# Norms between two layers: column sums with Newton steps, or sums on all partitions with Ln and Exp

## The chip, the cores and the metric

The kernel runs on one core of a Trainium2 chip. The metric is the device time of one execution in microseconds (us); lower is better. Times of three runs are shown, and one further execution was taken with the hardware profiler, which gives the trace.

Engines are called by their names here and by short names in the rows: TensorE (PE for its matmuls, PEld for its weight loads), VectorE (DVE), ScalarE (ACT), GpSimd (POOL) and SyncE (SP), whose queue issues most transfers. L318 is line 318 of the kernel before.

## The reference

The model has two layers (L = 2) over 512 tokens with 1,024 features each. With the parts that matter here:

```python
for l in range(DEPTH):
    shift, scale, gate = jnp.split(c_act @ w_ada[l] + b_ada[l], 3, axis=-1)
    h = rms_norm(x, norm_g[l]) * (1.0 + scale) + shift
    z = h @ w_in[l]          # queries, keys, values, forget gates, latents, gates
    ...                      # forgetting attention on 8 heads, latent attention on 8 heads
    y = concatenate([y_fox, y_mla]) @ w_out[l]
    x = x + gate * y
return rms_norm(x, final_g)
```

`rms_norm` multiplies each token by 1/sqrt(mean of its 1,024 squares + 1e-6). So between the layers the kernel has to finish the new x of a token, sum its squares over all features, take the root, scale x, and only then can it begin with the second layer's products for that token. The same sum is needed once more at the very end, for the last norm.

## The kernel before

**Layout.** x is kept transposed: 8 tiles, each with 128 features on the partitions and 512 tokens along the columns. Everything is float32. A product is made of three reduced-precision ones (`mm3`, L238): high weight part by high input part (L239), high by low (L240), low by high (L241); which of the operands is the weight differs between the output projection and the v projection. Each weight tile is loaded raw by SyncE (L220), its high part is a cast on ScalarE (L124), its low part a subtraction on VectorE (L127). High and low parts live in rings of three buffers each, raw weights in a ring of two, so a cast waits until TensorE has let go of the tile three places earlier.

**Between the layers.** `project` (L947) runs the output projection. Its tiles n = 0 to 3 are done on all 512 tokens, tiles 4 to 7 first on the tokens of the first half (`HALF[0]`), then on those of the second half in the order 7, 6, 5, 4; tiles 5 and 4 are loaded and split a second time for that. `tile_n` (L953) loads the old x as residual (L956), does 24 products (8 k steps by 3), adds gate times y to the residual (L962, VectorE), stores the new x (L965), and squares it (L317, ScalarE) and adds the square into `acc` (L318, VectorE). `half_done` is called once for each half. In layer 0 it is `enter_second` (L1003), in layer 1 `finish` (L1031).

`enter_second` sums `acc` over the partitions with 128-column weight loads and a one-column moving operand (L1014), so the sums come out with tokens on partitions. `newton` (L346) takes the root in twelve small operations on VectorE, a copy (L352) widens the result, and `spread` (L356) brings it back along the columns with one product for each 128 tokens (L361). Then `h_chunk` (L380) makes the second layer's input for each of 8 feature tiles: L385 on VectorE, L388 (high part) on ScalarE, L389 (low part) on VectorE; in the text these are the chunk operations. For the second half the sums stand after one step of the second layer's v projection on the first half's tokens (`v_half`, L509; SUMS_AT = 1), and the spread after two more (SPREAD_AT = 2). A step of `v_half` takes a pair of weight tiles, two k values by two token blocks by three products, 12 in all.

`finish` does the same for the last norm in another way: a matrix of ones as the weights' partner, so that every partition gets each token's sum (L1034, and L1036 for the last tile's square, which is not added into `acc`), then Ln (L1038) and Exp (L1039) on ScalarE, then multiplies and output transfers.

**What sets the order.** Inside `mix` (attention and input projections) TensorE's order is written out by hand. Everywhere else, and on all other engines, a planner orders the instructions: it goes through a simulated time and takes, of those that are ready, the one that stands earliest in the program. `keep_in_program_order` puts an instruction behind the one that precedes it in the program on its engine; it does not hold later ones back. Each engine works its list strictly in order. ScalarE needs a table load when it goes to a function that its present table lacks: Ln and Exp have one together, Tanh and Exp another.

Of the kernel before, what the change touches and what calls it, by code (L numbers as in the profile page):

```python
# [13 lines left out]
AF = mybir.ActivationFunctionType  # L14
# [3 lines left out]
P = 128  # L18
D = 1024
# [3 lines left out]
L = 2  # L23
# [41 lines left out]
V_LO = ('pvpp','pppv',)  # L65
ROWS_U = {1: 2}
PRIO_W = 0
SUMS_AT, SPREAD_AT = 1, 2
PIN_ROWS = (0,2,3,)
PE_ENGINE = mybir.EngineType.PE  # L70
FIRST_W = 816
# [9 lines left out]
HALF = (slice(0, 256), slice(256, 512))  # L81
# [3 lines left out]
def trunk(ctx, tc, xT_in, pos, c_in, cols_in, w_first, w_proj, w_small, w_v, w_uq, w_ukv, w_out, ada_0, ada_r, out):  # L85
    nc = tc.nc
# [17 lines left out]
    def nm(s):  # L104
        uid[0] += 1
        return f"{s}_{uid[0]}"

    def scr(tag="scr", bufs=4, dt=F32, n=T):
        return wk.tile([P, n], dt, tag=tag, bufs=bufs, name=nm(tag))
# [4 lines left out]
    def bank(kind):  # L114
        pool = {"p": ps_p, "s": ps_s, "t": ps_t, "a": ps_a}[kind]
        return pool.tile([P, T], F32, tag=kind, name=nm("ps" + kind))
# [20 lines left out]
    ones = const.tile([P, P], F32, name="ones")  # L137
# [5 lines left out]
    for half in range(2):  # L143
        cs = slice(512 * half, 512 * half + 512)
# [4 lines left out]
    eps_c = const.tile([P, 1], F32, name="eps_c")  # L149
# [68 lines left out]
    def load_w(src, n=1024):  # L218
        raw = wp.tile([P, 1024], F32, tag="raw", bufs=R_BUFS, name=nm("raw"))
        nc.sync.dma_start(out=raw[:, :n], in_=src)  # L220
        return raw

    def split_w(src, n=1024, eng=None):
        return parts_w(load_w(src, n), n, eng)
# [3 lines left out]
    def parts_w(raw, n, eng=None):  # L228
        with prio(boost[0]):
            lo = wp.tile([P, 1024], F32R, tag="wl", bufs=W_BUFS, name=nm("wl"))  # L230
            hi = wp.tile([P, 1024], F32R, tag="wh", bufs=W_BUFS, name=nm("wh"))
            ins = hi_of(hi[:, :n], raw[:, :n])
            if hold[0] and "w" in PIN_S:
                behind(ins, hold[0], "after the forget gates")
            lo_of(lo[:, :n], raw[:, :n], hi[:, :n], eng)
        return hi, lo
# [89 lines left out]
    def newton_steps(sums, cs, width):  # L326

        n = (cs.stop - cs.start) // P
        q = wk.tile([P, 4, NT], F32, tag="nw", bufs=3, name=nm("nw"))
        m, a, y, t = (q[:, i, 0:n] for i in range(4))  # L330
        for i, src in enumerate(sums):
            c = n // len(sums)
            nc.vector.tensor_scalar(out=m[:, i * c:(i + 1) * c], in0=src, scalar1=1.0 / width, scalar2=EPS,
                                    op0=ALU.mult, op1=ALU.add)

        nc.vector.tensor_scalar(out=y.bitcast(I32), in0=m.bitcast(I32), scalar1=-0.5, scalar2=float(0x5F3759DF),
                                op0=ALU.mult, op1=ALU.add)
        nc.vector.tensor_scalar(out=a, in0=m, scalar1=-0.5, scalar2=None, op0=ALU.mult)
        for _ in range(3):
            yield  # L340
            nc.vector.tensor_mul(out=t, in0=y, in1=y)
            nc.vector.tensor_mul(out=t, in0=t, in1=a)
            nc.vector.scalar_tensor_tensor(out=y, in0=t, scalar=1.5, in1=y, op0=ALU.add, op1=ALU.mult)
        yield y

    def newton(sums, cs, width):  # L346
        *_, y = newton_steps(sums, cs, width)
        return y, widen(y, (cs.stop - cs.start) // P)
# [7 lines left out]
    def spread(rb, cs, here=False):  # L356

        ps = bank("t")
        for j in range((cs.stop - cs.start) // P):
            s = slice(cs.start + j * P, cs.start + (j + 1) * P)  # L360
            mm = nc.tensor.matmul(out=ps[:, s], lhsT=rb[:, j * P:(j + 1) * P], rhs=ident, start=True, stop=True)  # L361
            if here and j == 0:
                tc.keep_in_program_order(mm)
        return ps
# [3 lines left out]
    class Layer:  # L368
# [578 lines left out]
        def project(self, half_done):  # L947
            l = self.l
            self.x = [slot(self.s_x + n) for n in range(KC)]
            sq = Squares()  # L950
            res_in = xT_in if l == 0 else x_dram

            def tile_n(n, w, cs, kind):  # L953
                c = cs.stop - cs.start
                res = scr(tag="gate", bufs=3)
                nc.sync.dma_start(out=res[:, :c], in_=res_in[:, n, cs])  # L956
                if n in self.part:
                    ps, w = self.part[n]
                else:
                    ps = bank(kind)  # L960
                self.out_mms(ps[:, :c], w, cs, range(EARLY_K if n in self.part else 0, KC))
                nc.vector.scalar_tensor_tensor(out=self.x[n][:, cs], in0=ps[:, :c], scalar=G_c[l][:, n:n + 1],  # L962
                                               in1=res[:, :c], op0=ALU.mult, op1=ALU.add)
                if l < L - 1:
                    nc.sync.dma_start(out=x_dram[:, n, cs], in_=self.x[n][:, cs])  # L965
                if n == 4 and l == L - 1 and cs is HALF[1]:
                    last = sq.last(self.x[n][:, cs], cs)
                else:
                    last = sq.add(self.x[n][:, cs], cs)
                if l == L - 1:  # L970
                    nc.scalar.mul(out=self.x[n][:, cs], in_=self.x[n][:, cs], mul=col(C_FG + n))
                return last

            w = {}

            def load(n):
                if n < 8 and n not in self.part:
                    w[n] = split_w(w_out[l, n])

            load(0)  # L980
            load(1)
            for n in range(8):
                load(n + 2)
                if n < 4:
                    tile_n(n, w.get(n), ALL, "p" if n < 2 else "s")
                    if l == 0:
                        ada_rest.step(ADA_P[n], self.spare)
                else:
                    tile_n(n, w[n], HALF[0], "p")
            half_done(0, sq.acc)  # L990
            for n in (7, 6, 5, 4):
                last = tile_n(n, w[n] if n > 5 else split_w(w_out[l, n]), HALF[1], "p")
            half_done(1, sq.acc, last)

    lay = [Layer(0, 8, 0, 8, 16, list(range(24, 48))),
# [4 lines left out]
        lay[0].start_first()  # L1000
    lay[0].mix(2, 2)

    def enter_second(half, acc, last=None):  # L1003
        if half == 0:
            lay[1].h_tiles()
            lay[1].v_tile()
        cs = HALF[half]
        v = lay[1].v_half(0)
        for _ in range(SUMS_AT if half else 0):
            next(v)  # L1010
        ps = bank("t")
        for j in range(2):
            t = slice(cs.start + j * P, cs.start + (j + 1) * P)
            mm = nc.tensor.matmul(out=ps[:, t.start:t.start+1], lhsT=acc[:, t], rhs=ones[:, 0:1], start=True, stop=True)  # L1014
            if half and j == 0:
                tc.keep_in_program_order(mm)
        _, rb = newton([ps[:, cs.start:cs.stop:P]], cs, D)
        for _ in range(SPREAD_AT if half else 0):
            next(v)
        r = spread(rb, cs, half == 1)  # L1020
        for k in range(KC):
            lay[1].h_chunk(k, cs, lay[0].x, r)
        if half == 1:
            for g in (v, lay[1].v_half(1)):
                for _ in g:
                    pass

    lay[0].project(enter_second)
    lay[1].mix(1, 1)

    def finish(half, acc, last=None):  # L1031
        cs = HALF[half]
        ps = bank("t")
        nc.tensor.matmul(out=ps[:, cs], lhsT=ones, rhs=acc[:, cs], start=True, stop=last is None)  # L1034
        if last is not None:
            nc.tensor.matmul(out=ps[:, cs], lhsT=ones, rhs=last[:, cs], start=False, stop=True)  # L1036
        r = scr(tag="aux", bufs=2)
        nc.scalar.activation(out=r[:, cs], in_=ps[:, cs], func=AF.Ln, scale=1.0 / D, bias=eps_c)  # L1038
        nc.scalar.activation(out=r[:, cs], in_=r[:, cs], func=AF.Exp, scale=-0.5)  # L1039
        o = [wk.tile([P, 3 * PT_J + T], F32, tag="pT", bufs=2, name=nm("o")) for _ in range(2)]  # L1040
        for ks in OUT_K:
            t = o[ks[0] // 6]
            for k in ks:
                at = 256 * (k % 6)
                (nc.gpsimd if k in OUT_POOL else nc.vector).tensor_mul(out=t[:, at:at + 256], in0=lay[1].x[k][:, cs],
                                                                       in1=r[:, cs])
            at = 256 * (ks[0] % 6)
            nc.sync.dma_start(out=out[:, ks[0]:ks[-1] + 1, cs],
                              in_=t[:, at:at + 256 * len(ks)].rearrange("p (k t) -> p k t", t=256))
# [74 lines left out]
```

## Time and profile before

| | us |
|---|---|
| three runs: median (lowest to highest) | 590.78 (589.86 to 594.66) |
| the profiled execution | 592.77 |
| its span, first to last instruction | 590.9 |

| engine | busy us | share of the span |
|---|---|---|
| TensorE matmuls | 555.6 | 94% |
| TensorE weight loads | 441.1 | 75% |
| VectorE | 440.3 | 75% |
| ScalarE | 368.6 | 62% |
| GpSimd | 33.0 | 6% |

The mean granted TensorE clock is 0.978 of full speed. Matmuls overlap, so a busy TensorE is not at its peak; a stop of TensorE shows as idle time in brackets ahead of an instruction, with the instruction that ended it. The stretch between the layers lies at about 290 to 333 us of the span.

### The profile page before, as it was taken

The page shows a single profiled execution, that of the slowest core. Times are in us where ns is not written, and L with a number is a line of the kernel's source. Part 1 is how long each engine was busy: PE and PEld are TensorE (multiplying, and loading weights), DVE is VectorE, ACT ScalarE, POOL GpSimd, SP SyncE. Part 2 cuts the span into 40 slices and gives each one's busy share as a digit, 9 for nine tenths or more (in the row PEclk, how much of TensorE's full clock was granted, in tenths as well). Part 3 has the DMA queues.
Part 4 walks back from the last instruction along what each step waited for, and adds up shares of the span by engine and source line. Part 5 has one row for each costly group of instructions (what it writes and reads, how often), then busy time and mean ns, then how long its engine had stood idle before and what let it go on. Part 6 is the DMA issues. An engine that isn't in the chain of part 4 may idle for free.

```text
span 590.9 us, 8588 instructions
## 1 busy us (share of the span) xinstructions
PE 555.6 (94%) x2942; PEld 441.1 (75%) x2942; DVE 440.3 (75%) x965; ACT 368.6 (62%) x783; POOL 33.0 (6%) x57
## 2 busy tenths in 40 slices
PE   7799989999899999999879999999999999899994
PEld 5477768777677767868777778877777777677893
DVE  2899776876858879788697677676597988864664
ACT  5344836676567879753356454576477777767643
POOL 4000110010001000000000030011001000000011
PEclk9799989999899999999999999999999999989998
DMA  8985144333314454778733315422132432341543
GB/s 284 404 293 177 39 129 154 102 123 108 90 37 119 125 158 143 258 242 272 226 101 122 108 41 150 133 76 74 54 108 86 100 104 76 100 126 36 158 139 113
DMA packets 36859, 81.08 MB, mean 137 GB/s; under 512 B 7616, under 2 KB 13760, under 8 KB 36816
## 3 DMA queue, kind: packets, MB, share of 16 engines
q1 hardware_dynamic: 35792, 80.28, 42.8%
q8 instruction: 23, 0.38, 0.3%
q0 software_dynamic: 1024, 0.27, 0.3%
q14 instruction: 20, 0.16, 0.1%
HBM read 72.36 MB, written 4.72 MB: 130 GB/s over the span
## 4 chain that ended last, share of the span: by engine, by line
PE 65%; DVE 15%; ACT 8%; DMA 8%; issue 3%; SPq 0%; DVEq 0%; ACTq 0%
PE psp L241 13%; PE psp L239 13%; PE psp L240 12%; PE psa L625 5%; PE pst L613 4%; PE pss L239 3%; DVE wl L127 3%; PE pss L240 3%; PE pss L241 3%; DMA raw<-in_w_out 3%; DMA scr<-mrow 3%; ACT wh L124 2%; PE pss L693 2%; DMA sl<-in_ada_r 2%; PE pss L694 1%
## 5 line engine op out<-in xcount | busy, mean ns | idle before, releaser
L239 PE MATMUL psp<-sl,wh 128*128 128x512 f32 (+1 forms) x488 | 188.5, 387 | 0.1
L241 PE MATMUL psp<-sl,wl 128*128 128x512 f32 (+1 forms) x488 | 179.7, 368 | 5.0 <-DVE wl L127 5.0
L240 PE MATMUL psp<-sl,wh 128*128 128x512 f32 (+1 forms) x488 | 179.1, 367 | 0.0
L241 PEld LDWEIGHTS psp<-sl,wl 128*128 128x128 f32 x488 | 93.0, 191 | 22.2 <-DVE wl L127 6.5
L239 PEld LDWEIGHTS psp<-sl,wh 128*128 128x128 f32 x488 | 93.4, 191 | 12.3 <-ACT vf L411 0.4
L240 PEld LDWEIGHTS psp<-sl,wh 128*128 128x128 f32 x488 | 93.6, 192 | 10.9
L127 DVE TENSOR_TENSOR wl<-raw,wh 128x1024 fp32r<-128x1024 f32 (+1 forms) x62 | 73.4, 1187 | 26.7 <-ACT wh L124 26.3
L124 ACT CAST wh<-raw 128x1024 fp32r<-128x1024 f32 (+1 forms) x63 | 63.6, 1014 | 36.8 <-PE psp L240 9.3
L601 ACT ACTIVATE p<-pss,st 128x128 f32<-128x128 f32 (+3 forms) x128 | 67.3, 527 | 25.9 <-DVE st L599 25.7
L604 ACT ACTIVATE p<-p,st 128x128 f32<-128x128 f32 (+3 forms) x128 | 70.8, 563 | 18.2 <-DVE st L602 17.8
L599 DVE TENSOR_REDUCE st<-pss 128x1 f32<-128x128 f32 (+3 forms) x128 | 61.9, 484 | 20.5 <-PE pss L695 13.2
L613 PE MATMUL pst<-ident,p 128*128 128x128 f32 x320 | 57.2, 277 | 0.7 <-ACT p L604 0.7
L619 ACT COPY pT<-pst 128x512 f32<-128x512 f32 (+2 forms) x72 | 31.5, 439 | 23.5 <-PE pst L613 22.8
L124 ACT CAST sl<-scr 112x512 fp32r<-112x512 f32 (+1 forms) x48 | 29.3, 616 | 20.8 <-DVE scr L631 15.7
L613 PEld LDWEIGHTS pst<-ident,p 128*128 128x128 f32 x320 | 38.0, 142 | 4.8 <-ACT p L604 1.3
L127 DVE TENSOR_TENSOR sl<-scr,sl 112x512 fp32r<-112x512 f32 (+1 forms) x48 | 32.7, 685 | 6.9 <-ACT sl L124 6.6
L602 DVE RECIPROCAL st<-st 128x1 f32<-128x1 f32 x128 | 19.7, 157 | 20.0 <-ACT p L601 19.4
L271 DVE SCALAR_TENSOR_TENSOR adr<-adr,cb 128x1024 f32<-128x1024 f32 x24 | 29.1, 1214 | 3.9 <-DMA adr<-in_ada_r 3.9
L239 PE MATMUL pss<-sl,sl 112*128 112x256 f32 (+2 forms) x64 | 23.3, 363 | 5.5 <-ACT p L601 5.5
L639 POOL DMA_DIRECT2D sl<-csq x16 | 9.2, 574 | 336.7 <-PE psp L241 166.6
L617 DVE COPY pT<-pst 128x384 f32<-128x384 f32 (+2 forms) x56 | 25.3, 451 | 0.4 <-PE pst L613 0.2
L388 ACT ACTIVATE sl<-scr,B 128x256 fp32r<-128x256 f32 (+1 forms) x24 | 13.1, 576 | 19.7 <-DVE scr L385 16.6
(197 smaller groups left out, 903.3 us busy)
## 6 DMA issues: line engine op xcount, KB each, us to landing
raw<-in_w_proj SPq DMA_DIRECT2D x36, 512.0 KB, 3.5
adr<-in_ada_r SPq DMA_DIRECT2D x24, 512.0 KB, 3.6
raw<-in_w_out SPq DMA_DIRECT2D x20, 512.0 KB, 4.1
sl<-in_w_v SPq DMA_DIRECT2D x16, 256.0 KB, 4.2
sl<-in_ada_r SPq DMA_DIRECT2D x16, 256.0 KB, 4.9
vm<-in_ada SPq DMA_DIRECT2D x6, 512.0 KB, 6.0
pT<-in_ada SPq DMA_DIRECT2D x6, 512.0 KB, 6.5
sl<-in_xT SPq DMA_DIRECT2D x8, 256.0 KB, 6.6
```

What stands on the lines that cost most here:

```text
L124: return nc.scalar.copy(out=dst, in_=src) if scale == 1.0 else nc.scalar.mul(out=dst, in_=src, mul=scale)
L127: (eng or nc.vector).tensor_sub(out=dst, in0=src, in1=hi.bitcast(F32))
L239: nc.tensor.matmul(out=ps, lhsT=lh, rhs=rh, start=first, stop=False)
L240: nc.tensor.matmul(out=ps, lhsT=lh, rhs=rl, start=False, stop=False)
L241: nc.tensor.matmul(out=ps, lhsT=ll, rhs=rh, start=False, stop=last)
L271: nc.vector.scalar_tensor_tensor(out=raw, in0=raw, scalar=0.5, in1=cb[:, cs], op0=ALU.mult, op1=ALU.mult, accum_out=dst)
L599: nc.vector.tensor_reduce(out=st[:, 0:1], in_=s[:, :w], op=ALU.max, axis=AX, negate=True)
L601: nc.scalar.activation(out=p[:, :w], in_=s[:, :w], func=AF.Exp, bias=st[:, 0:1], accum_out=st[:, 1:2])
L604: nc.scalar.mul(out=p[:, :w], in_=p[:, :w], mul=st[:, 2:3])
L613: nc.tensor.transpose(out=tp[:, j * P:(j + 1) * P], in_=p[:, j * P:(j + 1) * P], identity=ident)
L619: nc.scalar.copy(out=dst, in_=src)
L625: nc.tensor.matmul(out=ps[64 * a:64 * a + 64, j * P:T], lhsT=v[:, j, 64 * heads[a]:64 * heads[a] + 64], rhs=pTs[a][:, PT_J * j + P * j:PT_ ...
```

## The change

Between the layers the sums, the root and the spread are replaced by what `finish` did: both call one function `norms`. The last tile's square of the second half is now left out of `acc` in layer 0 too and goes into the sums as a second product. `norms` pins its first product behind the product before it in the program. The sums of the first half (in both layers) are called for after the second half's tile 7 instead of before it. For the second half they still stand after one step of the v projection, and nothing follows them before the chunk operations. A table load for Ln and Exp is put ahead of layer 0's output projection.

```diff
-SUMS_AT, SPREAD_AT = 1, 2
+SUMS_AT = 1
@@ project / tile_n
-                if n == 4 and l == L - 1 and cs is HALF[1]:
+                if n == 4 and cs is HALF[1]:
                     last = sq.last(self.x[n][:, cs], cs)
@@ project
-            half_done(0, sq.acc)
             for n in (7, 6, 5, 4):
                 last = tile_n(n, w[n] if n > 5 else split_w(w_out[l, n]), HALF[1], "p")
+                if n == 7:
+                    half_done(0, sq.acc)
             half_done(1, sq.acc, last)
@@ new, ahead of enter_second
+    def norms(acc, cs, last):
+        ps = bank("t")
+        mm = nc.tensor.matmul(out=ps[:, cs], lhsT=ones, rhs=acc[:, cs], start=True, stop=last is None)
+        tc.keep_in_program_order(mm)
+        if last is not None:
+            nc.tensor.matmul(out=ps[:, cs], lhsT=ones, rhs=last[:, cs], start=False, stop=True)
+        r = scr(tag="aux", bufs=2)
+        nc.scalar.activation(out=r[:, cs], in_=ps[:, cs], func=AF.Ln, scale=1.0 / D, bias=eps_c)
+        nc.scalar.activation(out=r[:, cs], in_=r[:, cs], func=AF.Exp, scale=-0.5)
+        return r
@@ enter_second
         for _ in range(SUMS_AT if half else 0):
             next(v)
-        ps = bank("t")
-        for j in range(2):
-            t = slice(cs.start + j * P, cs.start + (j + 1) * P)
-            mm = nc.tensor.matmul(out=ps[:, t.start:t.start+1], lhsT=acc[:, t], rhs=ones[:, 0:1], start=True, stop=True)
-            if half and j == 0:
-                tc.keep_in_program_order(mm)
-        _, rb = newton([ps[:, cs.start:cs.stop:P]], cs, D)
-        for _ in range(SPREAD_AT if half else 0):
-            next(v)
-        r = spread(rb, cs, half == 1)
+        r = norms(acc, cs, last)
         for k in range(KC):
             lay[1].h_chunk(k, cs, lay[0].x, r)
@@ ahead of layer 0's projection
+    tc.keep_in_program_order(nc.scalar.preload_act_table_set("natural_log_exp_and_others"))
     lay[0].project(enter_second)
@@ finish: the same five lines as in norms are taken out
+        r = norms(acc, cs, last)
```

## Rows read from the trace of the kernel before

**Rows 1.** the page, part 1: busy time, share of the span, instructions

```profile
PE 555.6 (94%) x2942; PEld 441.1 (75%) x2942; DVE 440.3 (75%) x965; ACT 368.6 (62%) x783; POOL 33.0 (6%) x57
```

**Rows 2.** timeline, TensorE: start, us, engine, line, operation, tiles, count [idle before it]

```profile
290.41 0.28 PE L239 MATMUL psp<-sl,wh 128*128 128x256 f32 x1
292.87 0.58 PE L1014 MATMUL pst<-ones,aux 128*128 128x1 f32 x4 [2.18 <-DVE aux L318]
293.31 0.36 PE L240 MATMUL psp<-sl,wh 128*128 128x256 f32 x1
...
294.46 0.28 PE L240 MATMUL psp<-sl,wh 128*128 128x256 f32 x1
...
307.88 0.50 PE L240 MATMUL pss<-wl,sl 128*128 128x512 f32 x1 [3.15 <-DVE wl L127]
...
311.44 0.85 PE L1014 MATMUL pst<-ones,aux 128*128 128x1 f32 x4
```

**Rows 3.** timeline, ScalarE, same columns: the cast that a weight buffer held up

```profile
294.82 1.05 ACT L124 CAST wh<-raw 128x1024 fp32r<-128x1024 f32 x1 [2.56 <-PE psp L240]
```

**Rows 4.** timeline, VectorE, 292 to 311 us

```profile
292.30 0.42 DVE L318 TENSOR_TENSOR aux<-aux,scr 128x256 f32<-128x256 f32 x1 [0.54 <-ACT scr L317]
...
298.20 1.26 DVE L385 SCALAR_TENSOR_TENSOR scr<-sl,A,pst 128x256 f32<-128x256 f32 x3 [0.87 <-PE pst L361]
...
307.14 0.68 DVE L127 TENSOR_TENSOR wl<-sl,wh 128x512 fp32r<-128x512 f32 x1
...
308.08 2.49 DVE L127 TENSOR_TENSOR wl<-sl,wh 128x512 fp32r<-128x512 f32 x4
```

**Rows 5.** windows: length, busy (instructions) by engine, clock, DMA share, GB/s

```profile
291.00:298.00 7.00, 5.03 (x41) 4.89 (x41) 4.74 (x18) 1.46 (x2) 0.00 (x0) 1.00 0.53 149
...
304.00:308.00 4.00, 0.85 (x6) 0.42 (x5) 3.96 (x10) 2.88 (x7) 0.00 (x0) 1.00 0.25 86
308.00:312.30 4.30, 4.30 (x15) 3.55 (x16) 2.57 (x5) 0.62 (x2) 0.00 (x0) 0.61 0.72 218
```

**Rows 6.** timeline, second layer's first-half sums on TensorE, then VectorE's first multiply

```profile
570.71 0.67 PE L1034 MATMUL pst<-aux,ones 128*128 128x256 f32 x2
571.03 0.47 PE L240 MATMUL psp<-sl,wh 128*128 128x256 f32 x1
...
572.38 3.20 DVE L1045 TENSOR_TENSOR o<-sl,aux 128x256 f32<-128x256 f32 x6 [1.81 <-ACT aux L1039]
```

**Rows 7.** timeline, TensorE, the v products of the second half

```profile
320.80 0.39 PE L241 MATMUL pss<-wh,sl 128*128 128x512 f32 x1
321.03 0.39 PE L239 MATMUL psp<-wh,sl 128*128 128x512 f32 x1
...
332.85 0.39 PE L241 MATMUL psa<-wh,sl 128*128 128x512 f32 x1
```

**Rows 8.** timeline, ScalarE: after layer 0's attention; a load in layer 1

```profile
266.67 2.00 ACT L124 CAST wh<-raw 128x1024 fp32r<-128x1024 f32 x2 [1.87 <-PE psp L240]
...
341.62 1.28 ACT L569 ACT_TABLE_LOAD   x1
```

**Rows 9.** timeline, VectorE: what waits for the logarithm

```profile
343.67 1.21 DVE L572 TENSOR_TENSOR_SCAN scr<-scr,scr 32x512 f32<-32x512 f32 x1 [2.73 <-ACT scr L569]
```

**Rows 10.** waits of TensorE from 333 us on: us in total, times, longest

```profile
PE psp L241 <- DVE wl L127: 0.9, 1, 0.9
```

**Rows 11.** one line's operations: count, ns min/median/max, first and last start

```profile
L385 DVE SCALAR_TENSOR_TENSOR scr<-sl,A,aux x8: 733/736/746, 18.7 to 54.1; 128x512 f32<-128x512 f32 x8
...
L723 DVE SCALAR_TENSOR_TENSOR lat<-lat,qgs,pst x4: 742/746/748, 157.1 to 440.1; 128x512 f32<-128x512 f32 x4
```

**Rows 12.** timeline, SyncE's queue, then VectorE: the second layer's end

```profile
573.43 2.54 SPq L1048 DMA_DIRECT2D out_T<-o  x4
576.08 0.45 SPq L956 DMA_DIRECT2D gate<-x_dram  x1
...
581.38 0.48 DVE L962 SCALAR_TENSOR_TENSOR sl<-psp,G,gate 128x256 f32<-128x256 f32 x1 [1.33 <-PE psp L241]
```

More of the change, by code (lines that the diff above doesn't have):

```diff
@@ L1032, in finish @@
         cs = HALF[half]
[L1033 to L1039, printed above, removed]
+        r = norms(acc, cs, last)
         o = [wk.tile([P, 3 * PT_J + T], F32, tag="pT", bufs=2, name=nm("o")) for _ in range(2)]
```

## The prediction

> **What bounds the kernel now.** I first read the shares of the page: TensorE is busy for 94% of the span, VectorE for 75% [rows 1]. So what can be won is TensorE's idle time, and a change between the layers is worth what it takes out of the stretch from 290 to 333 us. There I read TensorE's timeline. It stands twice. The first product after 290.41 us is the first half's column sums (L1014) at 292.87, after 2.18 us idle, which the last add into the squares (L318) ended; then the second layer's v product with a low weight part starts at 307.88, after 3.15 us idle behind VectorE's L127 [rows 2]. The rows on either side of the sums also show where they cut in. The product at 290.41 is an L239, and ScalarE's cast at 294.82 had waited for the buffer of tile 7's weights, whose last high product is the L240 at 294.46 [rows 2, 3]. From 293.31 to 294.46 at 0.12 us each are 10 products, with the last L241 11. So 11 of tile 7's 24 second-half products stand behind the sums, 13 before.
>
> VectorE's timeline explains the second stop. The first chunk operation of the first half (L385) starts at 298.20, that is 5.33 us after the sums began; then VectorE does 16 chunk operations, three adds of squares and three residual steps (L962), 22 in 8.94 us or 0.41 each, and only at 307.14 the low weight part (L127) that TensorE wants [rows 2, 4]. In the windows VectorE has 3.96 busy us of the 4.00 from 304 to 308, while TensorE has 0.85. The granted clock is 1.00 from 291 to 298, the stretch with the 2.18 us stop, and 0.61 from 308 to 312.3, behind the 3.15 us stop [rows 5]. So the longer stop took TensorE down towards the lower of its two levels (1.2 GHz) for a while, and the shorter did not.
>
> **The change, part by part.** *The sums one tile later.* The last add ends at 292.72 [rows 4], and nothing in the change makes it earlier, so the sums still begin at 292.87. But the 11 products come first, 1.32 us of work. The wait falls from 2.18 to about 0.9.
>
> *Ln and Exp instead of Newton and the spread.* The same three steps run at the second layer's end: from the sums' start (570.71) to VectorE's first multiply (572.38) are 1.67 us, and the two matmuls hold TensorE for 0.32 us (the next product starts at 571.03) [rows 6]. Now 5.33 us become 1.67: L385 starts at 292.87 + 1.67 = 294.54, 3.66 earlier. TensorE goes on at 293.19, does the 72 products of tiles 6, 5 and 4 (8.64 us) up to 301.83, and two products with a high part (0.46). VectorE does the same 22 operations, 8.94 us, then L127; from its start to TensorE's product were 0.74 us (307.14 to 307.88) [rows 2, 4]. So the low part is there at 294.54 + 8.94 + 0.74 = 304.2. The v products go on 3.7 us earlier, after a stop of about 1.9 us. ScalarE's cast for tile 4 starts at about 292.3, when the square before L318 is done, and ends at 293.4, ahead of Ln.
>
> *The clock.* A stop of 1.9 us is nearer the 2.18 that left the clock alone than the 3.15 that did not [rows 2, 5], so I take full clock. From 307.88 to 321.03 the rest of the first v half took 13.15 us with four sums and four spread products in it. 46 products at 0.23 us (320.80 to 321.03 [rows 7]) and four of the new sums at 0.16 make 11.2. That gives 1.9 more; if the clock falls all the same, about 0.3 of it is left, the spread's.
>
> *The second half.* Its Newton steps and widening go from VectorE too, as does one add: the last tile's square goes into the sums as a second pair of matmuls, the 0.64 us counted above. TensorE did not wait for this half's chunk operations: the second v half follows on at 321.03 right behind the product at 320.80, and takes 12.04 us to the end of the step at 332.85 [rows 7], some 11.0 of it products. I leave that stop of 1.0 us as it is; between none of it left and twice as long lies the bound.
>
> *The table.* A preload of the Ln and Exp table is added, behind layer 0's attention. There ScalarE sat idle for 1.87 us before the cast at 266.67, and a load lasts 1.28 [rows 8]; that idle time hides it, and without it the cast would be 1.28 us late. In layer 1 the load at 341.62 before the forget gates' Ln is not needed any more. VectorE waited 2.73 us for that Ln [rows 9], with weight parts queued behind, and TensorE waits 0.9 us for a weight part later [rows 10]. I take the 0.9 as gone; the bounds are 0 and 1.28.
>
> The Trainium skill, ScalarE: Activation LUTs, section What ACT_TABLE_LOAD costs, speaks against this part: a switch costs 1.28 us and a drain, about 2.66 together. By it the cast would be 0.8 us late in layer 0. The trace has 1.28 us from the load's start to the next operation, so the measured value stands.
>
> *Norms read from SBUF, not PSUM.* The chunk operation with both operands in SBUF took 736 ns for 512 columns, a like one with the norms in PSUM 746 [rows 11]. Nothing either way, at most 0.2 us over 16.
>
> *The second layer's end.* Its first sums also move behind tile 7. There they did not wait [rows 6], so TensorE's work is only reordered. With them go Ln, Exp, six multiplies on VectorE and two on POOL, and four output transfers on SyncE's queue at 573.43, 1.3 us later. Behind these stood the last tile's residual load at 576.08; TensorE, not this load, releases the last residual step at 581.38 [rows 12]. In the new order the residual step of tile 7 goes first, and with it that load's buffer. I take zero; with the load behind the outputs it starts 1.3 us later, still 4 us ahead of its use, so the bound is 0 to +1.
>
> Sum: 3.7 + 1.9 + 0.9 = 6.5 us. The profiled execution lasted 592.77 us (span 590.9), 2.0 above the median of 590.78: 586.3 by its own footing, 584.3 by the median's.
>
> **The rivals.** *One order slips* (loss of half the gain). VectorE does the low part of tile 4's weights after the 16 chunk operations, because these stand earlier in the program. It would be ready at 294.54 + 6.6 + 1.2 = 302.3; tile 4 wants it at 293.19 + 48 x 0.12 = 298.95. A stop of 3.3 us, the clock falls, the v products start at about 305.7 instead of 304.2: 1.5 + 1.9 lost, 587.7. For it speaks the priority, against it that the cast ends at 293.4, before the norms exist.
>
> *The second half's chunk operations push ahead of the first half's weights* (slower). The norms no longer wait for two further steps of weights, so these 16 operations come earlier in the program than the low parts of the second to fourth weight pair. If VectorE keeps that order, norms at 308.5 plus 6.6 plus 0.74 let TensorE go on at 315.8 instead of 307.6, at a lower clock; 34 products (7.8) and 1.9 for the clock bring it to 325.5, and with 12.04 to 337.5, 4.5 us later than now; less 0.9 for the table: 594.4. It decides once the second pair's low part is still undone when the norms arrive. Against it: VectorE had about 4 us between first low part and norms, and did four low parts in 2.49 us there [rows 4].
>
> *The gain is given back in layer 1*, where weights that arrive at their own time or another order on ScalarE and VectorE hold TensorE: 589.5. TensorE waits there only once on a projection's weight part, for 0.9 us [rows 10]; that speaks against it.
>
> *More is won*: the low parts slip in ahead of the residual steps, both stops by v vanish (1.9 and 1.0 more): 581.4.
>
> **How the numbers follow.** As summed 50%, one slip 20%, given back 10%, slower by order 10%, more 10%. The predicted time is 584.3; with its bounds the likeliest case runs from 582.5 to 586.5. The range from 581 to 590 takes in all but the slower case and the outer end of the best, and the terms' bounds. One per cent, 5.9 us, is about what a measurement of this kernel can tell from no change: 584.9 is the border. Two thirds of the likeliest case and the best case lie under it, 0.44; over 596.7 only the worst of the slower case, 0.05; the rest, 0.51, is within.
>
> **What would show it.** Right: no stop over 1.2 us at the first sums, L385 about 1.7 us after them, the first low v product about 11 us after them, granted clock 1.00 in the following 5 us, one load before the first tile of the projection and none at the forget gates. Wrong: a stop over 3 us by any low weight part with VectorE in chunk operations, or a first v half that ends at the old distance from 290.41.

## The result, and the profile after

The changed kernel took 581.59 us (median of four runs, 579.54 to 584.88) against 590.79 for the kernel before on the same chip (589.86 to 594.66); the ratio of the runs is 0.9856, with a 95% interval from 0.9811 to 0.9900. On another chip it took 582.61 (580.49 to 583.98), ratio 0.9867 [0.9836, 0.9898]. So the change wins about 1.4%, 8 us. The profiled execution lasted 580.7 us, its span 578.8.

The page's first part, engine by engine, answers to [rows 1]: VectorE has 27 instructions and 5 us less, ScalarE 4 more.

```profile
PE 552.0 (95%) x2932; PEld 438.7 (76%) x2932; DVE 435.2 (75%) x938; ACT 369.7 (64%) x787; POOL 32.7 (6%) x57
```

TensorE's timeline after (start, us, operation, tiles, count, in brackets the idle time before it) answers to [rows 2, 7].

```profile
292.24 0.67 PE L1007 MATMUL pst<-aux,ones 128*128 128x256 f32 x2 [1.20 <-DVE aux L318]
...
301.38 0.63 PE L239 MATMUL pss<-wh,sl 128*128 128x512 f32 x2
302.83 0.50 PE L240 MATMUL pss<-wl,sl 128*128 128x512 f32 x1 [0.82 <-DVE wl L127]
...
305.30 0.59 PE L1007 MATMUL pst<-aux,ones 128*128 128x256 f32 x2
305.73 0.59 PE L1010 MATMUL pst<-scr,ones 128*128 128x256 f32 x2
...
314.37 0.39 PE L239 MATMUL psp<-wh,sl 128*128 128x512 f32 x1
...
325.25 0.39 PE L249 MATMUL psp<-sl,wh 128*112 128x512 f32 x1
```

Two stops are left between the layers, 1.20 us at the first sums and 0.82 at the first low v product, where before there were 2.18 and 3.15. VectorE's timeline, the answer to [rows 4], shows why.

```profile
291.67 0.42 DVE L318 TENSOR_TENSOR aux<-aux,scr 128x256 f32<-128x256 f32 x1 [0.54 <-ACT scr L317]
292.01 0.48 DVE L962 SCALAR_TENSOR_TENSOR sl<-psp,G,gate 128x256 f32<-128x256 f32 x1
292.60 1.23 DVE L127 TENSOR_TENSOR wl<-raw,wh 128x1024 fp32r<-128x1024 f32 x1
293.75 0.42 DVE L318 TENSOR_TENSOR aux<-aux,scr 128x256 f32<-128x256 f32 x1
294.08 1.27 DVE L385 SCALAR_TENSOR_TENSOR scr<-sl,A,aux 128x256 f32<-128x256 f32 x3
...
302.09 0.68 DVE L127 TENSOR_TENSOR wl<-sl,wh 128x512 fp32r<-128x512 f32 x1
302.95 0.43 DVE L318 TENSOR_TENSOR aux<-aux,scr 128x256 f32<-128x256 f32 x1 [0.18 <-ACT scr L317]
303.29 4.30 DVE L127 TENSOR_TENSOR wl<-sl,wh 128x512 fp32r<-128x512 f32 x7
307.51 1.27 DVE L385 SCALAR_TENSOR_TENSOR scr<-sl,A,aux 128x256 f32<-128x256 f32 x3
```

The chunk operations begin 1.84 us after the sums instead of 5.33, with tile 4's low part (292.60) still ahead of them. All eight low parts of the first v half (302.09 and the seven from 303.29) stand ahead of the second half's chunk operations, which begin at 307.51. In the windows the clock is 1.00 at the first sums, as in [rows 5], and now also in the five microseconds from the first low v product on, where the kernel before had 0.66 (third row).

```profile
291.00:298.00 7.00, 5.80 (x47) 5.74 (x47) 6.34 (x15) 5.98 (x13) 0.00 (x0) 1.00 0.66 216
302.80:307.80 5.00, 4.97 (x22) 3.99 (x23) 4.85 (x9) 2.36 (x6) 0.00 (x0) 1.00 0.81 242
```

```profile
307.88:312.88 5.00, 5.00 (x17) 4.15 (x18) 3.25 (x7) 1.14 (x2) 0.00 (x0) 0.66 0.77 225
```

To compare executions I cut the time at four places of TensorE's order: the first sums, the first v product with a low weight part, the first product of the second v half, the small projection behind it (L249), and layer 1's first scores (L693). A last column runs from VectorE's residual step of tile 7's first half to those scores, so that it holds the wait at the sums as well. Marked (*): products of the second v half slipped ahead, so the two middle lengths are given together.

| kernel | sums to low v | to 2nd v half | to small proj. | to scores | sum | from tile 7 |
|---|---|---|---|---|---|---|
| before | 15.01 | 13.15 | 12.04 | 32.13 | 72.33 | 73.92 |
| before, once more | 16.18 | 13.15 | 12.04 | 32.12 | 73.49 | 75.08 |
| changed | 10.59 | 11.54 | 10.88 | 30.94 | 63.95 | 65.54 |
| changed, once more | 10.66 | 11.48 | 10.88 | 30.95 | 63.97 | 65.56 |
| e1_table | 16.16 | 14.31 | 12.07 | 30.95 | 73.49 | 75.08 |
| e2_late | 10.10 | 15.18 | 11.02 | 32.16 | 68.46 | 70.05 |
| e3_early | 14.86 | 11.53 | 10.88 | 30.94 | 68.21 | 69.80 |
| e4_nopre | 13.11 | 13.04 | 12.54 | 30.95 | 69.64 | 71.23 |
| e5_first | 10.59 | 11.85 | 12.06 | 30.94 | 65.44 | 67.03 |
| e6_second (*) | 10.11 | 26.49 | | 30.95 | 67.55 | 69.14 |
| e7_sums0 (*) | 10.99 | 23.10 | | 30.94 | 65.03 | 66.63 |
| e8_pool | 9.37 | 12.31 | 10.88 | 30.95 | 63.51 | 65.11 |
| e9_last0 | 11.26 | 11.49 | 10.88 | 30.94 | 64.57 | 65.44 |
| e10_both | 9.73 | 12.79 | 10.88 | 30.95 | 64.35 | 65.33 |

The change takes 8.38 us out of the last column (73.92 less 65.54), split as 4.42, 1.61, 1.16 and 1.19 over the four lengths. That agrees with the ratios of the runs, which come to 8.5 us on the one chip and 7.8 on the other; against the second execution of the kernel before it would be 9.5. The rest of the span differs by chance more than by the change, as the paragraph on the executions shows.

### The profile page after: what moved, and what is told of

The parts are those of the page before. It is cut to its first block, busy times and chain, and to the rows that moved or that the text cites. A ratio compares the mean times of both kernels' runs of the same rounds, so it can differ in the third digit from the quotient of the medians.

```text
span 578.8 us, 8543 instructions
## 1 busy us (share of the span) xinstructions
PE 552.0 (95%) x2932; PEld 438.7 (76%) x2932; DVE 435.2 (75%) x938; ACT 369.7 (64%) x787; POOL 32.7 (6%) x57
## 4 chain that ended last, share of the span: by engine, by line
PE 68%; DVE 13%; ACT 7%; DMA 7%; issue 3%; SPq 0%; POOL 0%; DVEq 0%; ACTq 0%; POOLq 0%
PE psp L239 13%; PE psp L241 13%; PE psp L240 13%; PE psa L625 5%; PE pst L613 4%; PE pss L239 3%; DMA scr<-mrow 3%; PE pss L241 3%; PE pss L240 3%; DVE wl L127 2%; DMA raw<-in_w_out 2%; PE pss L693 2%; ACT wh L124 1%; ACT p L601 1%; DVE st L599 1%
```

## The experiments

**The table alone.** The kernel before, with the Ln and Exp table loaded ahead of layer 0's projection and nothing else.

```diff
+    tc.keep_in_program_order(nc.scalar.preload_act_table_set("natural_log_exp_and_others"))
     lay[0].project(enter_second)
```

> The kernel before with nothing but the added table load ahead of layer 0's projection. Theory (the load in layer 1 was on the path): the stretch from the first product of proj_small (L249) to layer 1's first score (L693) falls from 32.1 us to 30.9, as in the changed kernel, and nothing else moves: about 589.6 us. Rival (the 1.2 us came from somewhere else in the change): 32.1 stays, 590.8 us.

Measured: 588.18 us (585.94 to 589.18, 7 runs; the kernel before 591.04 beside it), ratio 0.9939 [0.9918, 0.9961]. The length to the scores falls from 32.13 to 30.95, which is all that the changed kernel wins there; the load before the forget gates is gone. The first two lengths are 1.2 us longer each. The first of these also comes in the kernel before when it is run once more (16.18), so it is no effect of the load. The second goes with the clock, which was 0.50 in the five microseconds from the first low v product on. In this one execution the stretch as a whole is therefore no shorter (75.08, as in the kernel before once more). The ratio promises 3.6 us; beyond the 1.2 of the last length I can't place them.

**The later sums alone.** The new place, but with Newton steps and spread, and without the load.

```diff
-            half_done(0, sq.acc)
             for n in (7, 6, 5, 4):
                 last = tile_n(n, ...)
+                if n == 7:
+                    half_done(0, sq.acc)
```

> The kernel before with nothing but the first half's sums moved one tile later; Newton steps and spread stay. Theory (VectorE's chain from the sums to the first low v weights sets the time, not TensorE's wait at the sums): the wait at the sums falls from 2.2 to about 1.0 us, but the stop ahead of the first low v product grows by as much; from the sums to that product still 15.0 us, clock again about 0.6 behind it, time 590.8 us. Rival (the wait at the sums is worth itself): 1.2 us faster, 589.6.

Measured: 587.01 (583.07 to 590.92, 10 runs), ratio 0.9945 [0.9902, 0.9987]. The stretch is 3.9 us shorter, which neither theory had. VectorE's timeline shows where this comes from, and TensorE's what is given back.

```profile
294.14 0.69 DVE L127 TENSOR_TENSOR wl<-sl,wh 128x512 fp32r<-128x512 f32 x1
...
294.83 0.68 DVE L127 TENSOR_TENSOR wl<-sl,wh 128x512 fp32r<-128x512 f32 x1
...
296.97 0.48 DVE L385 SCALAR_TENSOR_TENSOR scr<-sl,A,pst 128x256 f32<-128x256 f32 x1 [0.87 <-PE pst L361]
```

```profile
305.81 0.50 PE L240 MATMUL pss<-wl,sl 128*128 128x512 f32 x1 [2.56 <-DVE wl L127]
```

The chunk operations start late (6.95 us after the sums), and in that time the first v pair's two low parts slip in between the Newton steps. So the first low v product doesn't wait at all, and the stop of 2.56 us comes at the second pair's. The product that waits comes 15.79 us after the sums, no sooner than in the kernel before (15.01), but 14 v products stand ahead of it where there were two. So the later place works through VectorE's order, not through TensorE's wait at the sums (0.94 us, as both theories had it). Behind the stop the clock stayed at 1.00, and 1.0 of the 3.9 us lies in the second v half; what the clock alone is worth here was not separated.

**Ln and Exp, with the sums at the old place.** The changed kernel with `half_done(0, sq.acc)` back ahead of the loop over tiles 7 to 4.

> The changed kernel with the first half's sums back ahead of the second half's tile 7; Ln and Exp, the table load and the rest stay. VectorE's list now has tile 4's low weight part behind the 16 chunk operations. Theory (the later place matters through that order, not through the wait at the sums): TensorE waits 3 to 5 us for tile 4's low part, the clock falls behind it, the first low v product comes 14 to 16 us after the sums instead of 10.6, time about 587 us. Rival (the later place is worth its 1.2 us of wait alone): 582.8 us, no stop at tile 4.

Measured: 585.66 (581.29 to 586.93, 5 runs), ratio 0.9895 [0.9848, 0.9943]. VectorE's list, then TensorE's stop:

```profile
295.06 1.67 DVE L385 SCALAR_TENSOR_TENSOR scr<-sl,A,aux 128x256 f32<-128x256 f32 x4 [1.82 <-ACT aux L1012]
...
302.91 1.21 DVE L127 TENSOR_TENSOR wl<-raw,wh 128x1024 fp32r<-128x1024 f32 x1
```

```profile
304.18 0.39 PE L241 MATMUL psp<-sl,wl 128*128 128x256 f32 x1 [2.35 <-DVE wl L127]
```

This is the order of the prediction's first rival: norms that are ready early put the 16 chunk operations ahead of tile 4's low part, and the projection itself stops for 2.35 us (3 to 5 expected). The first length is 14.86, hardly better than before and 4.3 longer than in the changed kernel; the other three are those of the changed kernel. Alone the later sums win 3.9 us of the stretch and Ln and Exp with their table 4.1, together 8.4: the early norms gain nothing in the first length until the sums stand behind tile 7.

**Without the load.** The changed kernel less the table load ahead of layer 0's projection.

> The changed kernel without the added table load: Ln and Exp of each half then get a load each (four of 1.28 us between the layers), and the one in layer 1 is back. Theory (the first half's norms are on the path, one for one): from the first sums to the first low v product 10.6 + 2.6 = 13.2 us, a stop of 3.4 us there, the clock falls behind it (1.6 us), layer 1 loses 1.2 again: about 587 us. Rival (the loads are hidden beside other work): only the 1.2 us in layer 1, 582.8 us.

Measured: 585.91 (584.10 to 589.13, 7 runs), ratio 0.9938 [0.9901, 0.9975]. ScalarE's timeline at the first sums; the same four rows come again from 309.36 on for the second half.

```profile
292.09 1.28 ACT L1012 ACT_TABLE_LOAD   x1
293.38 0.48 ACT L1012 ACTIVATE aux<-pst,eps_c 128x256 f32<-128x256 f32 x1
293.88 1.28 ACT L1013 ACT_TABLE_LOAD   x1
295.17 0.42 ACT L1013 ACTIVATE aux<-aux 128x256 f32<-128x256 f32 x1
```

```profile
304.42 0.50 PE L240 MATMUL pss<-wl,sl 128*128 128x512 f32 x1 [3.35 <-DVE wl L127]
```

Without the explicit load each Ln and each Exp gets a table load of its own, twice 1.28 us for each half. The stop by the first low part grows by 2.53 us, from 0.82 to 3.35, about the two loads of the first half, and the clock in the five microseconds behind it is 0.66. Against the changed kernel 2.5 us are lost up to that product, 1.5 behind it up to the second v half, both as expected, and 1.7 in the second v half, which the theory did not have. In all 5.7 us of the 8.4 hang on that one instruction. But the length to the scores stays at 30.95, although the load before the forget gates is back (338.55). I come back to that below.

**The halves apart.** First only the first half with Ln and Exp, then only the second.

```diff
 def enter_second(half, ...):
-    r = norms(acc, cs, last)
+    if half == 1:   # e5_first; half == 0 in e6_second
+        ...          # one-column sums, newton, spread as in the kernel before
+    else:
+        r = norms(acc, cs, last)
```

> The changed kernel with the second half's norms put back: one-column sums, Newton steps and spread products after two further v steps, its last square added into acc again. The first half keeps Ln and Exp and the later sums. Lengths are counted as: first sums to first low v product (10.59 us in the changed kernel, 15.01 before), from there to the second half's first product (11.54, 13.15), from there to the small projection (10.88, 12.04), from there to layer 1's first score (30.94, 32.13). Theory: the whole gain of the first stretch and of the clock comes from the first half; expected 10.6, 11.8 (the two spread products back, 0.3 less two sums), 12.0 (the second half's chunk operations stand behind the spread again and hold the last weights by about 1 us), 30.9: sum 65.3, about 583 us. Rival: each half brings about half of it, because VectorE's Newton steps of the second half push the low parts back too: sum 68, about 586 us.

> The changed kernel with the first half's norms put back to one-column sums, Newton steps and spread, at the later place; the second half keeps Ln, Exp and the second product pair. Theory: the first half as in the kernel with late sums alone, where sums to first low v product and from there to the second half's first product took 10.10 and 15.18 us with a stop of 2.56 at the second low part; I expect 25.0 for the two together, 10.9 for the second v half (its gain comes with its own Ln and Exp) and 30.9 after it: sum 66.8, about 585 us. Rival: the second v half's gain of 1.1 us is the first half's early low parts' doing and not the second half's norms': then 12.0 there, sum 68, about 586 us.

Measured: first half only 582.78 (578.30 to 585.01, 4 runs), ratio 0.9872 [0.9823, 0.9922]; second half only 585.75 (581.97 to 588.84, 10 runs), ratio 0.9925 [0.9897, 0.9953]. The first half's part brings 6.9 of the 8.4 us, all but the 1.2 of the second v half and 0.3 for the spread products, as expected to 0.2 us. The second half's part alone wins nothing over the later sums: its stretch is 0.9 us shorter than that of the later sums alone, and 1.2 of that is the last length, where this kernel has the table load. Its sum of 67.55 lies between theory (66.8) and rival (68) and decides nothing between them. Its TensorE and VectorE rows show what happens when the second norms come early and the first late:

```profile
305.77 0.67 PE L1007 MATMUL pst<-aux,ones 128*128 128x256 f32 x2 [2.04 <-DVE aux L318]
...
314.23 0.50 PE L240 MATMUL pss<-wl,sl 128*128 128x512 f32 x1 [1.41 <-DVE wl L127]
```

```profile
307.95 1.27 DVE L385 SCALAR_TENSOR_TENSOR scr<-sl,A,aux 128x256 f32<-128x256 f32 x3
...
313.50 0.68 DVE L127 TENSOR_TENSOR wl<-sl,wh 128x512 fp32r<-128x512 f32 x1
```

Six low parts were done when the norms arrived; the seventh stood behind 14 chunk operations, and TensorE stopped for it. That is the mechanism of the rival that I called slower, at a fraction of its price, because here only the last pair is hit.

**The second sums one step earlier.** In the changed kernel `SUMS_AT = 0`, to bring about that order on purpose.

> The changed kernel with the second half's sums ahead of the first v step instead of behind it. That is the rival of an order on VectorE in which the second half's 16 chunk operations come before low weight parts, made on purpose. Theory: TensorE then waits about 1.9 us at the second sums for the last square, and 1.0 to 1.5 us at a low part of a later pair, for which VectorE is late because of the chunk operations: 3 us longer from first sums to the small projection (36.0 against 33.0), while the rest stays, about 584.5 us. Rival: the sums are so short that their place doesn't matter, within 0.5 us of 33.0.

Measured: 584.05, one run. From first sums to the small projection 34.09 us against 33.01: 1.1 longer, not 3. TensorE did not wait at the second sums at all; it waited 1.22 us instead of 0.82 at the first low part and 0.45 at a later one, with five low parts done ahead of the chunk operations. The direction was right, the size a third.

**What is left.** The first v pair's low parts on GpSimd; tile 7's first-half square as a second pair of products; both.

```diff
-    lo_of(lo[:, s], raw, hi[:, s], nc.vector if V_LO[half][kp] == "v" else None)
+    lo_of(lo[:, s], raw, hi[:, s], nc.gpsimd if half == 0 and kp == 0 else nc.vector)
...
-                if n == 4 and cs is HALF[1]:
+                if (n == 4 and cs is HALF[1]) or (n == 7 and cs is HALF[0]):
```

> The changed kernel with the first v pair's two low parts on the idle GpSimd instead of VectorE. GpSimd takes 1.29 us for a subtraction-like operation of 128x512, and the casts before it end near 297. Theory: the stop of 0.82 us before the first low v product is what is left of VectorE being the bound of this stretch; here it vanishes and VectorE's later low parts come 0.6 to 1.2 us earlier, so first sums to first low v product becomes 9.6 to 9.8 us instead of 10.59, the rest stays, 580.6 us. Rival: GpSimd and VectorE disturb each other, VectorE's chunk operations grow from 0.40 each, and the stop stays.

> The changed kernel with tile 7's square of the first half fed to the sums as a second pair of products instead of added on VectorE first. Theory: the 1.20 us stop at the first sums, which that add ends, shortens by the add's 0.42 us, while two more products cost 0.24: 0.2 to 0.4 us gained between the last product before the sums and layer 1's first score. Rival: TensorE then waits for the square itself on ScalarE, and nothing is gained.

> Both together: first v pair's low parts on GpSimd, tile 7's first-half square as a second pair of products. Theory: the two stops that the change left, 1.20 and 0.82 us, go down to about 0.8 and 0, 1.0 to 1.3 us better than the changed kernel between the layers, 580.4 us. Rival: the v products are then held by the next pair's low parts, and no more than 0.3 us is left of it.

Measured: GpSimd 580.83 (579.90 to 581.85, 4 runs), ratio 0.9826 [0.9790, 0.9861]; the square 583.74, one run; both 580.37 (577.54 to 584.18, 6 runs), ratio 0.9826 [0.9785, 0.9867]. From tile 7 to the scores they are 0.4, 0.1 and 0.2 us shorter than the changed kernel. With the square as a product the sums come 0.87 us after tile 7's residual step instead of 1.59, but the first low v product still comes 12.13 us after it (12.18 in the changed kernel), since VectorE's low part is no sooner. With GpSimd's parts the first low v product no longer waits, but the add into the squares is late instead, and TensorE waits at the second sums (first row GpSimd's alone, second both):

```profile
306.07 0.67 PE L1007 MATMUL pst<-aux,ones 128*128 128x256 f32 x2 [0.51 <-DVE aux L318]
```

```profile
303.60 0.67 PE L1007 MATMUL pst<-aux,ones 128*128 128x256 f32 x2 [0.97 <-DVE aux L318]
```

Of the 1.0 to 1.3 us that I expected of the combination 0.2 came. That is the size of the rival, but not its mechanism: what holds TensorE is the wait at the second sums and not a low part. Both beat the kernel before by 1.7%; that they beat the changed kernel is not shown, the intervals overlap.

**The executions.** Both kernels once more, unaltered.

> The changed kernel once more, unaltered, as a measure of what differs from run to run. Theory: lengths between the layers (10.59, 11.54, 10.88, 30.94) come out within 0.3 us of these, while layer 1's attention, 173.61 us with the same order of instructions as before the change (175.25), comes out between 171.6 and 175 for reasons of the run alone. Rival: attention is 173.6 again within 0.2, so that its 1.6 us belong to the change.

> The kernel before once more, unaltered, for what differs from one profiled execution to the next. Theory: the lengths between the layers come out again as 15.01, 13.15, 12.04 and 32.13 us within 0.5 each, since they follow from orders and waits, while layer 1's attention, 175.25 us with a stop of 1.89 us in the first execution, comes out near the 171.6 to 173.6 of the other kernels, and the sums start up to 3 us elsewhere than at 292.87. Rival: attention is 175 us again, so that the change does win time there, in a way that the order of instructions doesn't show.

Measured: the changed kernel's four lengths repeat within 0.07 us. The kernel before took 589.66 in one run, and its lengths repeat within 0.01 except the first, 16.18 against 15.01. There the clock fell behind a wait at the sums that was shorter than the first time; TensorE, then two windows ahead of and behind the sums:

```profile
290.95 0.58 PE L1014 MATMUL pst<-ones,aux 128*128 128x1 f32 x4 [1.44 <-DVE aux L318]
```

```profile
288.00:290.95 2.95, 1.51 (x13) 1.33 (x12) 1.78 (x5) 0.83 (x2) 0.00 (x0) 1.00 0.77 237
290.95:294.00 3.05, 3.05 (x17) 3.05 (x18) 1.35 (x10) 0.19 (x1) 0.00 (x0) 0.60 0.39 130
```

Layer 1 from its first scores to the first residual step of its projection took 181.35 us in the first execution of before, with a stop of 1.89 us and a slice of clock 0.91, and 178.99 in the second; the two of the changed kernel took 178.52 and 179.03. So nothing is won there. (The 175.25 and 173.61 of the expectations ran to the last L625 row. A row can stand for several like instructions, so that mark moves; by it the second execution of before gave 175.36, and the rival would stand. The residual step is one instruction and the better mark.) The start of the first residual step in layer 0 lies between 264.9 and 270.5 us in the 14 executions, most of which share their order up to there: 5.5 us of chance, more than half of what the change is worth. The kernel's end, from layer 1's first residual step on, is 44.35 and 44.37 before, 44.09 and 44.10 changed.

## Why the prediction was right, and where its sizes were not

The forecast was 584.3 us in a range from 581 to 590, by 6.5 us out of the stretch. The time of 581.6 lies in it, 9.2 us under the runs of before; the stretch gave 8.4. So the likeliest case held in its mechanism. In size the time lies 0.9 us under that case's own lower bound of 582.5, beside the 581.4 of the rival in which more is won. But that rival's order did not come: the first low part (302.09) still stands behind the three residual steps, the last two of which start from 301.31. What the stretch gave beyond the sum, 1.9 us, is the four terms below; the other 0.8 us is within what the runs of one kernel differ by.

- *The first stop, 3.7 expected, 4.4 measured.* The chunk operations began 1.84 us after the sums (1.67 expected) and TensorE followed VectorE's low part by 0.74 us, as read. Mis-sized was VectorE's work between: 22 operations in 8.94 us were carried over from [rows 4], but there were 20 in 8.01 us, because one add went ahead of the chunk operations and one behind the low part. The stop that was to be 1.9 us was 0.82. The wait at the sums was 1.20 and 0.44 us in the two executions (0.9 expected).
- *The clock, 1.9 expected, 1.6 measured.* The clock stayed at 1.00, as said; from low v product to second half are 11.54 us against the 11.2 worked out. With the first half's norms alone it stays up too (1.00).
- *The second v half, 0 expected, 1.16 measured.* This step failed. I left its stop of 1.0 us as it was, with none of it left as a bound. The halves apart show what it hung on: 12.06 with Newton and spread in the second half, 10.88 with Ln and Exp. With Ln and Exp the chunk operations begin 6.86 us ahead of the second v half (307.51 and 314.37) and no longer hold up the last low parts. In the kernel before they began 2.55 us ahead of it (318.48 and 321.03), a low part stood among them, and TensorE stopped for that:

```profile
318.48 1.26 DVE L385 SCALAR_TENSOR_TENSOR scr<-sl,A,pst 128x256 f32<-128x256 f32 x3 [0.94 <-PE pst L361]
...
324.24 0.68 DVE L127 TENSOR_TENSOR wl<-sl,wh 128x512 fp32r<-128x512 f32 x1
```

```profile
324.98 0.50 PE L240 MATMUL psp<-wl,sl 128*128 128x512 f32 x1 [0.62 <-DVE wl L127]
```

- *The table, 0.9 expected, 1.19 measured.* The size held, the reason only half. I had it that the load in layer 1 makes VectorE late. The run without the preload has that load, and yet no wait. What differs is VectorE's order, here in the kernel before, then in the run without the preload:

```profile
352.19 0.68 DVE L681 TENSOR_TENSOR sl<-psp,sl 64x512 fp32r<-64x512 f32 x1
...
353.36 1.23 DVE L127 TENSOR_TENSOR wl<-raw,wh 128x1024 fp32r<-128x1024 f32 x1
```

```profile
349.00 1.21 DVE L127 TENSOR_TENSOR wl<-raw,wh 128x1024 fp32r<-128x1024 f32 x1
350.25 0.68 DVE L681 TENSOR_TENSOR sl<-psp,sl 64x512 fp32r<-64x512 f32 x1
```

  The low part now stands ahead of the first L681 and is in time. The same order comes with the preload alone, so the preload and Ln with Exp each suffice to turn it; the later sums alone do not (32.16, with the old order). Whether the load's removal in the old order would have done so as well was not run.
- *Hidden work.* The preload lies at 264.44 to 265.72, and the cast behind it still waits 0.46 us for TensorE: it costs nothing, as said. The norms from SBUF cost nothing either: L385 takes 476 ns on average, before it took 474. The end gained 0.26 us, where 0 to +1 was given.
- *The prediction's test of a page.* That a table switch costs about 2.66 us, as the Trainium skill has it (ScalarE: Activation LUTs, What ACT_TABLE_LOAD costs), is not what these runs show: the four loads of the run without the preload take 1.28 us each, and the next operation starts 1.29 to 1.30 us after the load's start. No drain shows ahead of a load either: the one at 293.88 starts 0.02 us behind the end of the Ln (293.38 and 0.48).
- *The rivals.* One order slips: it is what happens with the sums at the old place (a stop of 2.35 us). Slower by order: in the changed kernel all eight low parts stand ahead of the chunk operations; the order came in part with Newton in the first half (a stop of 1.41 us) and with the second sums one step earlier (0.45). Given back in layer 1: no, the length to the scores is shorter by 1.19, and the rest of layer 1 no longer; the 589.5 of this rival had no sum behind it.

One premise of the prediction fell: that a stop of about 2 us leaves the clock alone and one of about 3 does not. Stops of 2.18, 2.11 and 2.56 us were followed by 1.00, but one of 1.44 by 0.60 and one of 2.35 by 0.66. So the 1.9 us of the clock came right on a rule that these runs don't bear out, and luck has a part in it. Behind the stops that came, 0.82 and 0.89 us in the two executions, the clock stayed up; that it would have behind the 1.9 us forecast is not shown.

## What to carry to other kernels

Where a planner orders the other engines, shortening a chain also moves everything that was ordered by its lateness: ask which work slipped in while the chain was slow, and place the chain's start so that this work is still ahead of it. Price a moved step by counting the instructions that will really stand between it and the one that the bottleneck waits for. And profile the kernel before twice, since one execution's stops and clock can be a few microseconds of chance.

## What the runs showed of the hardware

GpSimd's two subtractions of 128x512 took 4.38 and 1.48 us, where I had taken 1.29 from its other work. Around the change from the first to the second, two of VectorE's chunk operations took 2.43 us, which take 0.88 elsewhere, and ended at 303.87, by 0.28 us behind GpSimd's last. GpSimd's tile view (shortest, median, longest in ns) and VectorE's timeline:

```profile
L127 POOL TENSOR_TENSOR wl<-sl,wh x2: 1480/2930/4379, 297.8 to 302.1; 128x512 fp32r<-128x512 f32 x2
```

```profile
301.44 2.43 DVE L389 SCALAR_TENSOR_TENSOR sl<-scr,B,sl 128x256 fp32r<-128x256 f32 x2
```

Each thus seems to have held the other up. The Trainium skill (SBUF — State Buffer, Who interferes with whom) says that a VectorE instruction with two inputs in SBUF contends with a GpSimd one that reads SBUF. Both rows agree with that. They do not show that the one that starts first holds up the other for its whole length: GpSimd's first subtraction was under way from 297.77, and VectorE's chunk operations beside it kept their length (1.27 us for three) until VectorE went on to a residual step at 300.90, with one operand from PSUM; the subtraction ended 1.25 us after that.

The clock behind a stop is not settled by the stop's length. TensorE's wait for a low part was 2.56 us with the sums late and 2.35 with Ln and Exp at the old place; here the five microseconds behind each:

```profile
305.80:310.80 5.00, 5.00 (x24) 4.19 (x25) 4.77 (x15) 1.14 (x2) 0.00 (x0) 1.00 0.71 228
```

```profile
304.18:309.18 5.00, 5.00 (x26) 4.84 (x27) 3.71 (x8) 0.90 (x2) 0.00 (x0) 0.66 0.71 230
```

What does settle it, no run here tells.
